# A tuned single-core hybrid layer: operand splits moved, the first norm's outputs shared with POOL, and the last sum kept in PSUM

## The chip, the cores and the metric

The kernel runs on one core of a Trainium2 chip. The metric is the device time of one execution in microseconds (us). Of the kernel before, three runs gave 1477.32, 1479.01 and 1482.19 us; the median is 1479.01. Engines are named as in the profile: PE is TensorE (PEld its weight load), DVE is VectorE, ACT is ScalarE, POOL is GpSimd, SP is SyncE, which here issues DMAs.

## The reference

One post-norm layer on x of 1024 tokens by 2048 channels, all in float32:

```python
h = einsum('bsd,dc->bsc', x, w_in) + b_in                   # 2048 -> 4352 columns
q, k, v, g_attn, u_pool, g_pool = split(h)                  # 1024, 128, 128, 1024, 1024, 1024
a = banded_sink_attention(q, k, v, sinks, bias, valid) * silu(g_attn)   # 16 heads of 64, 2 kv heads, window 128
b = multiscale_pool(u_pool, w_pool, pool_scale) * silu(g_pool)          # trailing means over 2, 4, 8, 16
mix = einsum('bsc,cd->bsd', concatenate([a, b]), w_out)     # 2048 -> 2048
ple = sigmoid(einsum('bsd,de->bse', x, w_gate_ple)) * einsum('bsp,pd->bsd', p, w_ple)
out = layer_norm(DEEPNORM_ALPHA * x + mix + ple, ln_gain, ln_bias)
```

The three large products (34 blocks of 128 columns for `w_in`, 16 for `w_gate_ple`, 16 for `w_out`, each over 2048 channels) are nearly all of the arithmetic. `ple` is a per-layer embedding: p has 256 channels.

## The kernel before

**Layout.** Everything is kept transposed: channels on the 128 partitions, tokens along the free axis, in two halves of 512 tokens.

**Products.** A float32 operand is split into a high part (a cast on ACT, `copy`, L728) and a low part (a subtraction on DVE, `lo`, by the helper at L125). A product is then three matmuls, high by high, low by high and high by low (`mm3`, L182 to L184). A weight of 128x512 split this way is a unit (`wh`, `wl`), made four ahead of its use from a ring of five raw tiles.

**Jobs.** The large products run as Strassen-like jobs, each for two blocks of outputs and half of the contraction. A job has seven smaller products over the operands `b11`, `b21`, `t1`, `t2`, `t3`, `b22`, `t4` (h for high, l for low); the t operands are sums and differences of raw blocks (`two`), built on DVE. Results gather in `part` tiles: ACT copies the first product of a bank (L402), DVE adds the others from the PSUM banks `qa`, `qb` and `sc`. Two or three jobs share one set of operands and are a group; a product of one job is 12 matmuls of 512 columns. The operands of a group come from `set_from` (raw x), from `set_kept` (differences kept in DRAM), or from other sums.

**The order of the work.** `run_group` runs the products of a group one after another; each is a step of a clock. `after(n, f)` and `later(n, f)` place a piece of work n ticks on, and the scheduler then puts the instructions into each engine's queue. So a tick sets the place in a queue and not a time.

**The stages.** s1 to s4 are the projections from x, in which the heads of the attention run beside s2. The first group of s1 runs while x and the first weights are still being loaded; the embedding products of four early blocks (`EARLY`) stand among its products: `ple_split(n)` splits a block's embedding weights into `t3h` and `t3l` (L767), p lies split in `t4h` and `t4l`, and `ple_half(n, h)` is a turn of 12 matmuls, six in each of the banks `tr` and `pv`, whose results ACT copies to `b22h` or `b22l` as storage. `v_build` (L522) brings the values V, fetched from DRAM, to the form that the attention needs, with transposes on PE. s5 is the output projection for 768 tokens; s6 is eight plain jobs (`run_plain`, units a11 to a22, no Strassen) for the other 256, with operands split from `rest_x`.

**The norm.** Weights of `w_out` are centred over output channels, and `less_mean` (L905) adds what is left of the mean, so that the norm needs only the mean of squares. `norm_square` squares a block on ACT (L915), `norm_sums` adds squares with PE (L924), `norm_scale` forms the reciprocal root, which matmuls with ones spread over the partitions (L931 in `norm_spread` for the 768 tokens, L957 for the 256), and `norm_out` multiplies each of 16 blocks by it on DVE, scales and shifts it on ACT (`ident_act`, L128) and stores it. The first norm (`one`, 768 tokens) runs beside s6. The second (`two`, 256 tokens) ends the kernel: `norm_out_two` (L975) does two blocks at a time.

**Queues.** Loads go through SP (`load`, L139) and stores and other DMAs through POOL (`aside`, L144). POOL also does the masks (L612), some softmax additions, and accumulating DMAs (L415).

Of the kernel before, what the change touches and what calls it, by code (L numbers as in the profile page):

```python
# [64 lines left out]
class Layer:  # L65
# [265 lines left out]
    def set_kept(self, get, keep):  # L331

        r = {}

        def fetch(i):
            if i < 7:
                u = UNITS[BESIDE[i]]
                h, k = int(u[2:] or 1) - 1, 2 * (int(u[1]) - 1)
                r[u] = []
                for n in range(2):  # L340
                    src = keep[u][n] if u in keep else get(h, k + n)
                    r[u] += [self.fetch(src[:, m]) for m in range(2)]

        def step(i):
            u = UNITS[BESIDE[i]]
            self.split_unit(u, r.pop(u))
            fetch(i + 2)

        def begin():
            self.F = T  # L350
            fetch(0)
            fetch(1)

        return [begin] + [lambda i=i: step(i) for i in range(7)]
# [123 lines left out]
    def run_plain(self, g):  # L478

        (job,), order = self.groups[g]  # L480
        for i in range(2):
            ps = self.bank(BANKS[0][i], 2)[:, :F2]
            for u in range(2):
                wh, wl = self.take()
                for k in range(4):
                    f = slice(k * P, (k + 1) * P)
                    mm = self.mm3(ps, (wh[:, f], wl[:, f]), self.x_plain(4 * u + k), u + k == 0, False)
                if u:
                    mm = self.less_mean(ps, F1)
                self.mark("PE", mm)  # L490
                self.feed_raw()
                if u:
                    t = self.new_part(job.b[i])
                    self.add_to(t, ps, False)
                    job.done(job.b[i], t)
# [18 lines left out]
    def v_build(self, g, src):  # L514
# [12 lines left out]
        for h in range(2):  # L527
            self.ident_act(src[h], src[h], self.c(C_BIN + VB))
            self.after(2 + (1 + 4 * g) * h, lambda h=h: build(h))
# [240 lines left out]
    def ple_half(self, n, h, tags):  # L770

        i = EARLY[n]
        if n > 1 and not h:
            self.ple_split(n)
# [184 lines left out]
    def norm_out(self, L, j):  # L959
        d = L["d"].pop(j)  # L960
        self.tt(d, d, L["a"], ALU.mult)
        self.ident_act(d, d, self.c(C_B + j), self.c(C_G + j))
# [19 lines left out]
    def run(self):  # L982
# [77 lines left out]
        s6 = [Job(w, b0, b1, 0, None, lambda b, c: self.second_done(b, c), F2, plain=True) for w, b0, b1 in centred]  # L1060
        for j in s4[-2:]:
            j.wait = 6
# [42 lines left out]
        def first(fetch, r):  # L1105
# [11 lines left out]
            piece(s1[2], 0, up)  # L1117
            fetch("b12")
# [3 lines left out]
            self.ple_load(3)  # L1122
# [21 lines left out]
        self.run_group(0, steps, before=lambda *at: at in turn and self.ple_half(*turn[at], (("tr", 1), ("pv", 1))))  # L1144
# [22 lines left out]
        def build_kv(b, build, group):  # L1167
            src = [self.slot()[:, :T] for h in range(2)]
            for h in range(2):
# [9 lines left out]
        self.after(t + 63 + 22, lambda: build_kv(VB, self.v_build, 1))  # L1179
# [116 lines left out]
        self.first_done = first_done  # L1296
        for i in range(n5):
            self.run_group(g + i)
# [3 lines left out]
        hi, lo = ([self.tile(self.xp[u], [P, 4, half], f"{u}{s}", F32R).rearrange("p k t -> p (k t)") for u in ("b11", "b21")] for s in "hl")  # L1302
        for k in range(4):
            r = rest_x[k]
            f = slice((k % 2) * 2 * F2, (k % 2) * 2 * F2 + 2 * F2)
            h, l = (t[k // 2][:, f].rearrange("p (k t) -> p k t", k=2) for t in (hi, lo))
            nc.scalar.copy(out=h, in_=r)
            self.lo(l, r, h)
# [28 lines left out]
        self.later(3, lambda: self.norm_scale(one, 2))  # L1337
        for j in range(NB):
            self.later(6 + 18 * j // 16, lambda j=j: self.norm_out(one, j))
# [4 lines left out]
        for i, d in enumerate(pair):  # L1344
            self.norm_out_two(two, 2 * i, d, (nc.gpsimd, None, nc.gpsimd, nc.vector, nc.gpsimd, None, nc.gpsimd, nc.vector)[i])
# [55 lines left out]
```

## Time and profile before

| view | number |
|---|---|
| median of the runs | 1479.01 us |
| profiled execution | 1477.94 us, span 1476.2 us |
| PE busy | 1439.7 us, 98% of the span |
| DVE busy | 1123.1 us, 76% |
| ACT busy | 788.4 us, 53% |
| POOL busy | 295.8 us, 20% |
| mean granted clock of PE | 0.993 |

A row of the timeline has the start, the duration, the engine, the line, the operation, output and inputs by their names, the shape, a count, and in brackets how long the engine had been idle before it and what released it. A row of the waits has what waited for what, the sum of the waits, their number and the longest. Short rows of one engine overlap a little at their ends, since they are pipelined.

### The profile page before, as it was taken

How to read it: one execution, taken by the hardware profiler on the slowest of the kernel's cores; microseconds unless marked ns; L12 is line 12 of the kernel's file. 1: busy time of each engine (PE TensorE's matmuls, PEld its weight loads, DVE VectorE, ACT ScalarE, POOL GpSimd, SP SyncE). 2: the span in 40 equal slices, each digit the busy share in tenths (PEclk: the TensorE clock that was granted, in tenths of full speed). 3: DMA queues.
4: the chain of work that ended last, by engine and by line, in shares of the span. 5: the costliest groups of instructions: out<-in, count | busy, mean ns of one | idle time of the engine just before them, and what ended most of it. 6: DMA issues, size and time to landing. Idle time of an engine off the chain costs nothing. (4 is left out here: it accounts for less than half of the span.)

```text
span 1476.2 us, 20532 instructions
## 1 busy us (share of the span) xinstructions
PE 1439.7 (98%) x6928; PEld 1217.1 (82%) x6928; DVE 1123.1 (76%) x2033; ACT 788.4 (53%) x1566; POOL 295.8 (20%) x412
## 2 busy tenths in 40 slices
PE   8899999999999999999999999999999999999996
PEld 7788888888888788888788778788877888899995
DVE  6758577888788888888777786767678566987786
ACT  6535456655666566565655354433356433554475
POOL 1000113233233232324011111111011111111232
PEclk9899999999999999999999999999999999999998
DMA  9364687454445554466765759899699678595465
GB/s 350 145 215 170 164 230 232 145 170 165 158 173 181 185 169 171 172 214 218 205 198 133 207 160 307 288 266 289 196 320 301 168 190 231 138 258 126 120 239 200
DMA packets 109993, 301.35 MB, mean 204 GB/s; under 512 B 12544, under 2 KB 18048, under 8 KB 109888
## 3 DMA queue, kind: packets, MB, share of 16 engines
q1 hardware_dynamic: 84672, 217.46, 42.9%
q0 software_dynamic: 21888, 75.25, 21.0%
q10 hardware_dynamic: 3328, 7.34, 1.5%
q8 instruction: 54, 0.88, 0.2%
q14 instruction: 51, 0.42, 0.1%
HBM read 205.62 MB, written 94.37 MB: 203 GB/s over the span
## 5 line engine op out<-in xcount | busy, mean ns | idle before, releaser
L728 ACT CAST wh<-raw 128x512 fp32r<-128x512 f32 x428 | 264.1, 619 | 401.5 <-PE qa L183 132.5
L125 DVE TENSOR_TENSOR wl<-raw,wh 128x512 fp32r<-128x512 f32 x428 | 300.3, 705 | 111.2 <-ACT wh L728 105.4
L402 ACT COPY part<-qa 128x512 f32<-128x512 f32 (+1 forms) x180 | 103.9, 577 | 75.0 <-PE qa L184 74.0
L612 POOL TENSOR_SCALAR_AFFINE_SELECT s<-s 128x512 fp32r<-128x512 f32 x128 | 102.1, 809 | 132.2 <-ACT s L605 96.6
L125 DVE TENSOR_TENSOR part<-part,qb 128x512 f32<-128x512 f32 (+1 forms) x120 | 81.0, 675 | 44.9 <-PE qb L184 38.7
L182 PE MATMUL qa<-b11h,wh 128*128 128x512 f32 (+2 forms) x292 | 109.3, 374 | 0.4 <-ACT wh L728 0.4
L182 PE MATMUL qb<-b21h,wh 128*128 128x512 f32 (+2 forms) x292 | 109.1, 374 | 0.0
L184 PE MATMUL qa<-b11h,wl 128*128 128x512 f32 (+2 forms) x292 | 108.9, 373 | 0.0
L183 PE MATMUL qa<-b11l,wh 128*128 128x512 f32 (+2 forms) x292 | 108.8, 373 | 0.0
L184 PE MATMUL qb<-b21h,wl 128*128 128x512 f32 (+2 forms) x292 | 108.7, 372 | 0.0
L183 PE MATMUL qb<-b21l,wh 128*128 128x512 f32 (+2 forms) x292 | 108.5, 372 | 0.0
L182 PE MATMUL qa<-t2h,wh 128*128 128x512 f32 (+1 forms) x260 | 100.9, 388 | 3.3 <-ACT wh L728 2.1
L182 PE MATMUL qb<-t1h,wh 128*128 128x512 f32 (+1 forms) x260 | 101.2, 389 | 2.3 <-ACT t2h L728 1.4
L182 PE MATMUL qa<-t4h,wh 128*128 128x512 f32 (+1 forms) x260 | 100.4, 386 | 2.4 <-DVE part L125 2.4
L182 PE MATMUL qa<-t3h,wh 128*128 128x512 f32 (+1 forms) x260 | 100.6, 387 | 1.8 <-ACT part L402 1.8
L184 PE MATMUL qa<-t2h,wl 128*128 128x512 f32 (+1 forms) x260 | 100.1, 385 | 1.6 <-DVE wl L125 1.6
L182 PE MATMUL qb<-b22h,wh 128*128 128x512 f32 (+1 forms) x260 | 100.2, 386 | 0.0
L183 PE MATMUL qb<-t1l,wh 128*128 128x512 f32 (+1 forms) x260 | 100.0, 385 | 0.0
L184 PE MATMUL qb<-t1h,wl 128*128 128x512 f32 (+1 forms) x260 | 100.0, 385 | 0.0
L184 PE MATMUL qb<-b22h,wl 128*128 128x512 f32 (+1 forms) x260 | 99.8, 384 | 0.0
L183 PE MATMUL qa<-t3l,wh 128*128 128x512 f32 (+1 forms) x260 | 99.7, 384 | 0.0
L183 PE MATMUL qb<-b22l,wh 128*128 128x512 f32 (+1 forms) x260 | 99.7, 383 | 0.0
(325 smaller groups left out, 3577.1 us busy)
## 6 DMA issues: line engine op xcount, KB each, us to landing
raw<-in_win SPq DMA_DIRECT2D x65, 512.0 KB, 4.3
h<-part SPq DMA_DIRECT2D x34, 512.0 KB, 2.9
part<-h POOLq DMA_DIRECT2D x34, 512.0 KB, 6.6
cw<-in_wout SPq DMA_DIRECT2D x64, 256.0 KB, 3.0
raw<-in_wgate SPq DMA_DIRECT2D x32, 512.0 KB, 4.9
raw<-wc SPq DMA_DIRECT2D x32, 512.0 KB, 4.4
s<-in_x SPq DMA_DIRECT2D x44, 256.0 KB, 5.6
wc<-cw SPq DMA_DIRECT2D x32, 256.0 KB, 2.4
```

Source lines behind the costliest of these rows:

```text
L125: return (eng or self.nc.vector).tensor_tensor(out=out, in0=a, in1=b, op=op)
L182: mm(ps, wh, xh, start=start, stop=False, skip_group_check=True)
L183: mm(ps, wh, xl, start=False, stop=False, skip_group_check=True)
L184: return mm(ps, wl, xh, start=False, stop=stop, skip_group_check=True)
L402: self.mark("ACT", self.nc.scalar.copy(out=dst, in_=ps))
L612: nc.gpsimd.affine_select(out=o4, in_=a4, pattern=[[0, 4], [sign, P]], compare_op=ALU.is_ge, fill=0.0, base=0 if side else -1, channel_mul ...
L728: ins = self.nc.scalar.copy(out=out, in_=a)
```

## The change

Seven edits stand in one diff:

- **A, early units.** The 512 KB load for the early blocks 2 and 3 is issued ahead of the loads of `b12`, the raw weights and `b22`, and `ple_split(2)` and `ple_split(3)` are issued before the second product of the first group, not at the turns that use them.
- **B, values.** V of the second kv group is fetched and transposed in two halves, at 17 and 24 ticks; before, both were fetched at 22.
- **C, operand steps.** In `set_kept` a step other than the first splits two of its four pieces at once, and the other two, with the fetch of a later operand, a tick later.
- **D, last operand.** The operand of s6 is split during the last group of s5, piece by piece, and not after it.
- **E, first norm.** `norm_scale`'s second argument, the ticks from it to the matmuls that spread the reciprocal root (`norm_spread`), is 3 instead of 2; the outputs come at 7 + 17j // 16 instead of 6 + 18j // 16, and the scale and shift of odd blocks are one POOL instruction each (128x768) where ACT had one.
- **F, last sum.** In the last plain job the second block's partial sum is added to PSUM by a matmul with the identity; ACT squares from PSUM and DVE copies it out, where DVE added the partial sum first.
- **G, last outputs.** In `norm_out_two` the odd blocks are all scaled and shifted by POOL, where POOL had four, DVE two and ACT two of them.

```diff
@@ set_kept
         def step(i):
             u = UNITS[BESIDE[i]]
-            self.split_unit(u, r.pop(u))
-            fetch(i + 2)
+            pieces = r.pop(u)
+            self.split_unit(u, [])
+            for n in range(2):
+                self.split_part(u, n, pieces[n])
+            def rest():
+                for n in range(2, 4):
+                    self.split_part(u, n, pieces[n])
+                fetch(i + 2)
+            if i:
+                self.after(1, rest)
+            else:
+                rest()
@@ run_plain
+            final = job.mean and i
...
+                if final and not u:
+                    t = self.new_part(job.b[i])
+                    nc.tensor.matmul(ps, self.ident, t, start=False, stop=False, skip_group_check=True)
                 if u:
                     mm = self.less_mean(ps, F1)
...
-                if u:
+                if u and final:
+                    job.done(job.b[i], ps)
+                    nc.vector.tensor_copy(out=t, in_=ps)
+                elif u:
                     t = self.new_part(job.b[i])
                     self.add_to(t, ps, False)
                     job.done(job.b[i], t)
@@ v_build
-        for h in range(2):
+        for h in src:
             self.ident_act(src[h], src[h], self.c(C_BIN + VB))
-            self.after(2 + (1 + 4 * g) * h, lambda h=h: build(h))
+            self.after(2 + h * (g == 0), lambda h=h: build(h))
@@ ple_half
-        if n > 1 and not h:
-            self.ple_split(n)
@@ norm_out
         self.tt(d, d, L["a"], ALU.mult)
-        self.ident_act(d, d, self.c(C_B + j), self.c(C_G + j))
+        if j % 2:
+            self.nc.gpsimd.tensor_scalar(out=d, in0=d, scalar1=self.c(C_G + j), scalar2=self.c(C_B + j), op0=ALU.mult, op1=ALU.add)
+        else:
+            self.ident_act(d, d, self.c(C_B + j), self.c(C_G + j))
@@ the first loads
+            self.ple_load(3)
             fetch("b12")
             for job in s1[1:3]:
                 piece(job, 1, all_)
             fetch("b22")
-            self.ple_load(3)
@@ the first group
-        self.run_group(0, steps, before=lambda *at: at in turn and self.ple_half(*turn[at], (("tr", 1), ("pv", 1))))
+        def early(*at):
+            if at in turn:
+                self.ple_half(*turn[at], (("tr", 1), ("pv", 1)))
+            elif at == (1, 0):
+                self.ple_split(2)
+                self.ple_split(3)
+        self.run_group(0, steps, before=early)
@@ beside s2
-        self.after(t + 63 + 22, lambda: build_kv(VB, self.v_build, 1))
+        for h in range(2):
+            self.after(t + 63 + 17 + 7 * h, lambda h=h: build_kv(VB, self.v_build, 1, (h,)))
@@ s5
+        def last_operand(k):
...
+            nc.scalar.copy(out=h, in_=rest_x[k])
+            self.lo(l, rest_x[k], h)
         for i in range(n5):
+            if i == n5 - 1:
+                for k in range(4):
+                    self.later(5 + 2 * k, lambda k=k: last_operand(k))
             self.run_group(g + i)
-        for k in range(4):
...
-            nc.scalar.copy(out=h, in_=r)
-            self.lo(l, r, h)
@@ s6 and the norms
-        self.later(3, lambda: self.norm_scale(one, 2))
+        self.later(3, lambda: self.norm_scale(one, 3))
         for j in range(NB):
-            self.later(6 + 18 * j // 16, lambda j=j: self.norm_out(one, j))
+            self.later(7 + 17 * j // 16, lambda j=j: self.norm_out(one, j))
...
-            self.norm_out_two(two, 2 * i, d, (nc.gpsimd, None, nc.gpsimd, nc.vector, nc.gpsimd, None, nc.gpsimd, nc.vector)[i])
+            self.norm_out_two(two, 2 * i, d, nc.gpsimd)
```

In the first group, DVE's queue around the split `t3l` stands so before (`two` and `raw` are sums of operand blocks and weights, `t1l` the low part of operand t1, `wl` a weight's):

```order
L125 TENSOR_TENSOR raw_298<-raw_297,raw_298 128x512
L125 TENSOR_TENSOR wl_577<-s_212_571,wh_576 128x512
L125 TENSOR_TENSOR raw_297<-s_212_571,raw_297 128x512
L125 TENSOR_TENSOR t3l_338<-two_334,t3h_337 128x512
L125 TENSOR_TENSOR raw_297<-raw_297 128x512
L125 TENSOR_TENSOR two_325<-two_331,two_325 128x1024
L125 TENSOR_TENSOR wl_623<-raw_293,wh_622 128x512
L125 TENSOR_TENSOR t3l_338<-two_334,t3h_337 128x512
L125 TENSOR_TENSOR two_523<-two_330,two_308 128x1024
```

and with the change, up to the first half of the sum for t2 (`two_527`):

```order
L125 TENSOR_TENSOR b21l_458<-two_319,b21h_457 128x1024
L125 TENSOR_TENSOR wl_482<-raw_295,wh_481 128x512
L125 TENSOR_TENSOR t3l_338<-two_324,t3h_337 128x512 x2
L125 TENSOR_TENSOR two_308<-two_326,two_308 128x1024
L125 TENSOR_TENSOR wl_500<-raw_297,wh_499 128x512
L125 TENSOR_TENSOR two_309<-two_327,two_309 128x1024
L125 TENSOR_TENSOR t1l_522<-two_308,t1h_521 128x1024
L125 TENSOR_TENSOR raw_293<-raw_293 128x512
L125 TENSOR_TENSOR t1l_522<-two_309,t1h_521 128x1024
L125 TENSOR_TENSOR wl_535<-s_183_443,wh_534 128x512
L125 TENSOR_TENSOR two_527<-two_332,two_308 128x1024
```

Both halves of `t3l` moved from behind the weight work of the third product to ahead of the sums for t1.

On POOL, behind the reciprocal root of the first norm (`st`), there were only the DMAs of the outputs (`d`, two for each block):

```order
L125 TENSOR_TENSOR st_13467<-st_13467,mhalf 128x6
L144 DMA out<-d_12195 128x512
L144 DMA out<-d_12195 128x256
L144 DMA out<-d_12196 128x512
L144 DMA out<-d_12196 128x256
L144 DMA out<-d_12197 128x512
```

and now each odd block has its scale and shift there too:

```order
L125 TENSOR_TENSOR st_13467<-st_13467,mhalf 128x6
L144 DMA out<-d_12195 128x512
L144 DMA out<-d_12195 128x256
L981 TENSOR_SCALAR d_12196<-d_12196,cst 128x768
L144 DMA out<-d_12196 128x512
L144 DMA out<-d_12196 128x256
L144 DMA out<-d_12197 128x512
```

Eight such instructions of 128x768 stand in POOL's queue, the last in front of the last output of the first norm.

On PE, in s2, the transposes of V (`sc<-ident`) stood at the end of the product over t4, in front of the next group's `b11`:

```order
L184 MATMUL qa_4684<-t4h_1509,wl_4789 128x512
L603 MATMUL tr_4909<-ident,s_4552 128x128 x2
L603 MATMUL tr_4909<-ident,s_4627 128x128 x2
L522 MATMUL sc_4934<-ident,s_4760 128x128 x4
L182 MATMUL qa_4948<-b11h_1273,wh_4829 128x512
```

and now those of the first half stand in front of the product over t2, some 80 rows earlier:

```order
L184 MATMUL qb_4712<-b21h_1279,wl_4605 128x512
L587 MATMUL sc_4737<-kh_1759,s_4674 128x256
L587 MATMUL sc_4737<-kl_1760,s_4674 128x256
L587 MATMUL sc_4737<-kh_1759,s_4675 128x256
L587 MATMUL sc_4737<-kl_1760,s_4675 128x256
L542 MATMUL sc_4744<-ident,s_4577 128x128 x4
L182 MATMUL qa_4687<-t2h_1377,wh_4642 128x512
```

More of the change, by code (lines that the diff above doesn't have):

```diff
@@ L478, in run_plain @@
     def run_plain(self, g):
+        nc = self.nc
         (job,), order = self.groups[g]
@@ L1060, in run @@
         s6 = [Job(w, b0, b1, 0, None, lambda b, c: self.second_done(b, c), F2, plain=True) for w, b0, b1 in centred]
+        s6[-1].mean = True
         for j in s4[-2:]:
@@ L1165, in run, with build_kv @@
         self.kv = self.work_pool("kv", 1, over)
-        def build_kv(b, build, group):
-            src = [self.slot()[:, :T] for h in range(2)]
-            for h in range(2):
+        def build_kv(b, build, group, halves=(0, 1)):
+            src = {h: self.slot()[:, :T] for h in halves}
+            for h in halves:
                 self.aside(src[h], kvd[b][:, h * T : h * T + T])
@@ L1296, in run @@
         self.first_done = first_done
+        hi, lo = [], []
+        def last_operand(k):
+            if k % 2 == 0:
+                for t, s in ((hi, "h"), (lo, "l")):
+                    u = ("b11", "b21")[k // 2]
+                    t.append(self.tile(self.xp[u], [P, 4, half], f"{u}{s}", F32R).rearrange("p k t -> p (k t)"))
+            f = slice((k % 2) * 2 * F2, (k % 2) * 2 * F2 + 2 * F2)
+            h, l = (t[k // 2][:, f].rearrange("p (k t) -> p k t", k=2) for t in (hi, lo))
+            nc.scalar.copy(out=h, in_=rest_x[k])
+            self.lo(l, rest_x[k], h)
         for i in range(n5):
+            if i == n5 - 1:
+                for k in range(4):
+                    self.later(5 + 2 * k, lambda k=k: last_operand(k))
             self.run_group(g + i)
         g += n5
-        hi, lo = ([self.tile(self.xp[u], [P, 4, half], f"{u}{s}", F32R).rearrange("p k t -> p (k t)") for u in ("b11", "b21")] for s in "hl")
-        for k in range(4):
-            r = rest_x[k]
-            f = slice((k % 2) * 2 * F2, (k % 2) * 2 * F2 + 2 * F2)
-            h, l = (t[k // 2][:, f].rearrange("p (k t) -> p k t", k=2) for t in (hi, lo))
-            nc.scalar.copy(out=h, in_=r)
-            self.lo(l, r, h)
         self.x_plain = lambda k: tuple(t[k // 4][:, (k % 4) * F2 : (k % 4) * F2 + F2] for t in (hi, lo))
```

## The prediction

> **What bounds the kernel now.** First the page's head, then the waits, then PE's timeline at each long wait, last the busy times in short windows.
>
> ```profile
> span 1476.2 us, 20532 instructions
> PE 1439.7 (98%) x6928; PEld 1217.1 (82%) x6928; DVE 1123.1 (76%) x2033; ACT 788.4 (53%) x1566; POOL 295.8 (20%) x412
> ...
> PE tr L184 <- DVE t3l L125: 5.3, 1, 5.3
> PE tr L182 <- ACT t3h L767: 2.3, 1, 2.3
> PE pv L625 <- DVE v L125: 1.7, 1, 1.7
> ```
>
> PE is busy for 1439.7 of 1476.2 us, so this change can win only PE's idle time (36.5 us), the clock lost beside it, and the tail; three single waits are 9.3 us of it. It loses wherever another engine, late, makes PE wait. The two longest waits stand in the first group, with a slowed clock behind them:
>
> ```profile
> 33.09 0.39 PE L184 MATMUL sc<-b21h,wl 128*128 128x512 f32 x1
> 35.75 0.50 PE L182 MATMUL tr<-t4h,t3h 128*128 128x512 f32 x1 [2.28 <-ACT t3h L767]
> 42.26 0.80 PE L184 MATMUL tr<-t4h,t3l 128*128 128x512 f32 x1 [5.31 <-DVE t3l L125]
> 60.40 0.39 PE L182 MATMUL tr<-t4h,t3h 128*128 128x512 f32 x1
> 63.12 0.39 PE L182 MATMUL qa<-t2h,wh 128*128 128x512 f32 x1
> ...
> 36.00:40.00 4.00, 0.95 (x4) 0.42 (x3) 4.00 (x8) 0.91 (x3) 1.46 (x1) 0.70 0.59 199
> 40.00:44.00 4.00, 1.74 (x4) 1.46 (x5) 4.00 (x7) 0.45 (x1) 0.00 (x0) 0.50 0.00 0
> 44.00:48.00 4.00, 4.00 (x11) 3.10 (x11) 3.93 (x5) 2.42 (x4) 0.00 (x0) 0.52 0.52 210
> ```
>
> A window row has the stretch, its length, the busy time (and count) of PE, PEld, DVE, ACT and POOL, then PE's granted clock, the DMA share and GB/s. The clock's mean over 36 to 40 is 0.70 and over the next 4 us 0.50: full for (0.70 - 0.50) / 0.50 x 4 = 1.6 us, then half, so it fell at 37.6. By the same working it rose 0.2 us before 48. That is 10.2 us at half speed, begun 4.1 us after the steady work ended at 33.5.
>
> **A, the early units** (`ple_split(2)` and `(3)` sooner, the 512 KB load for them ahead of b12). Before, DVE is full up to 44, and t3l is one of its last steps:
>
> ```profile
> 26.21 1.23 DVE L125 TENSOR_TENSOR two<-two,two 128x1024 f32<-128x1024 f32 x1 [3.02 <-DMA two<-in_x]
> 29.70 2.36 DVE L125 TENSOR_TENSOR t1l<-two,t1h 128x1024 fp32r<-128x1024 f32 x2
> 41.52 0.68 DVE L125 TENSOR_TENSOR t3l<-two,t3h 128x512 fp32r<-128x512 f32 x1
> ...
> 27.47 1.05 ACT L728 CAST t1h<-two 128x1024 fp32r<-128x1024 f32 x1 [2.29 <-DVE two L125]
> 44.80 0.59 ACT L728 COPY b22h<-tr 128x512 f32<-128x512 f32 x1 [4.35 <-PE tr L184]
> ...
> GB/s 350 145 215 170 164 230 232 145 170 165 158 173 181 185 169 171 172 214 218 205 198 133 207 160 307 288 266 289 196 320 301 168 190 231 138 258 126 120 239 200
> ```
>
> On SP's queue the load is moved past b12, the raw weights of two jobs and b22. It lands where b12 did, at 26.2, and each of those lands one slot later, 524 KB at the first slice's 350 GB/s, 1.5 us. DVE had stood idle for b12 for 3.02 us; now the t3l pair runs from 26.8 to 28.0, and that covers the slot (b12 is there at 27.7). So t3h and t3l are ready long before 33.3. The price is a later t2: from 26.21 up to its second half DVE's new queue holds ten 128x512 steps and six of 128x1024. Back to back a row's span overlaps the next by about 0.08, which leaves 0.60 of 0.68 and, for the two t1l, 2.28 / 2 = 1.14: 6.0 + 6.8 = 12.8, up to 39.05.
>
> PE then runs: p2 ends at 33.1 + 0.2 = 33.3 (matmuls stream every 2.72 / 12 = 0.227 us, from 60.40 to 63.12). Four turns of 12 early matmuls and three jobs of the third product are 7 x 2.72 = 19.1. Two waits stay: the first job's bank, which DVE's `part<-part,qb` frees at 36.2 (0.2), and the second turn's bank `tr`: its copy stands on ACT behind the cast of t2's second half, 39.05 + 1.05 + 0.59 = 40.7, where PE asks at 36.2 + 2.7 = 38.95 (1.75). The fourth product starts at 33.3 + 19.1 + 0.2 + 1.75 = 54.4 instead of 63.12: **-8.7**. Weights don't bound that stretch: the units are made four ahead, 4 x 2.7 us, and raw lands 1.5 us later. Bounds: 33.3 + 19.1 = 52.4 gives -10.7; if 1.75 us of idling drops the clock once more for 10.2 us, half of that goes, 5.1: -3.6.
>
> The trace has 2.28 idle us, 1.2 us of matmuls, and the second wait from 42.26 - 5.31 = 36.95; the clock fell 0.65 us into that one. The Trainium skill, page "TensorE: Matmul & The Clock Gate", section "Part 1: The HAM clock gate", has the clock halved after an idle window of about 3.4 us; the trace agrees no further than that 4.1 us with little work were enough. By that rule 1.75 us would not trip it.
>
> **B, values** (halves of V fetched at ticks 17 and 24, not both at 22; transposes about 80 PE rows earlier) and **C, operand steps** (two pieces now, two a tick later):
>
> ```profile
> 489.24 0.47 PE L625 MATMUL pv<-s,v 128*128 128x256 f32 x2 [1.75 <-DVE v L125]
> ...
> 705.21 0.68 DVE L125 TENSOR_TENSOR part<-part,qb 128x512 f32<-128x512 f32 x1
> 706.04 0.47 PE L182 MATMUL qb<-t1h,wh 128*128 128x512 f32 x1 [1.38 <-ACT t2h L728]
> ```
>
> B: 80 matmuls at 0.227 are 18 us, ten times the wait, so v is there: **-1.75**. The transposes themselves stand on PE ahead of that stretch's products; if their source comes late they stop those, and the bound is 0. C: the cast named is long done; the bank is free when the DVE row above ends at 705.89. In the new order one 128x512 step (0.60) fewer stands ahead of it: **-0.65** (0 to -1.4).
>
> **D, last operand** split during the group before. ACT and DVE do the same eight steps earlier, in a stretch where PE's waits are short:
>
> ```profile
> 1387.68 0.44 PE L182 MATMUL qb<-t1h,wh 128*128 128x384 f32 x1 [0.82 <-DVE d L125]
> ```
>
> By the new order PE comes to this wait without two matmuls of 384 columns that had run ahead (2 x 0.227 x 384 / 512 = 0.34), and the bank comes about as late, perhaps 0.1 sooner: **+0.2** (-0.8 to +1).
>
> **E, the first norm.** All 16 outputs are multiplied on DVE; the scale and shift of the eight odd ones go from ACT to POOL, in place, 128x768 in SBUF. That stretch:
>
> ```profile
> 1421.00:1434.00 13.00, 13.00 (x112) 13.00 (x112) 12.99 (x22) 12.27 (x20) 6.34 (x12) 1.00 0.81 275
> 1434.00:1450.00 16.00, 15.51 (x125) 14.71 (x124) 16.00 (x28) 14.99 (x23) 8.90 (x17) 1.00 0.98 356
> ...
> 1444.86 0.68 DVE L125 TENSOR_TENSOR wl<-raw,wh 128x512 fp32r<-128x512 f32 x1
> 1445.59 0.38 PE L184 MATMUL qb<-b11h,wl 128*128 128x256 f32 x1
> ```
>
> DVE is the bound here, not ACT: it is busy for 28.99 of 29 us, and PE takes `wl` 0.05 us after DVE writes it (1445.54, 1445.59). So ACT's eight steps fewer gain nothing (27.3 of 29 us busy, it keeps pace), and a microsecond that DVE loses is one that PE loses. On POOL's queue each step stands ahead of the DMA issues of its output, for which no engine waits. DVE's own work stays; but POOL costs DVE time where both read SBUF:
>
> ```profile
> 318.53 0.75 POOL L125 TENSOR_TENSOR s<-s 128x256 f32<-128x256 f32 x1 [6.88 <-ACT s L583]
> 319.51 0.91 POOL L125 TENSOR_TENSOR s<-s 128x256 f32<-128x256 f32 x1 [0.23 <-ACT s L583]
> 318.79 1.04 DVE L125 TENSOR_TENSOR wl<-raw,wh 128x512 fp32r<-128x512 f32 x1
> 319.75 0.69 DVE L125 TENSOR_TENSOR st<-st 128x2 f32<-128x2 f32 x1
> ```
>
> The DVE subtraction, 0.68 elsewhere, lasts 1.04 beside the first POOL step, and a step of 128x2 lasts 0.69, up to where the second ends (320.42, 320.44). They take turns. What such a POOL step takes itself:
>
> ```profile
> 1466.69 0.56 POOL L975 TENSOR_SCALAR t1h<-t1h,cst 128x256 f32<-128x256 f32 x1 [2.64 <-DVE t1h L125]
> 1.18 0.29 POOL masks.py:199 TENSOR_SCALAR_AFFINE_SELECT ident<-ident 128x128 f32<-128x128 f32 x1
> 455.30 0.64 POOL L612 TENSOR_SCALAR_AFFINE_SELECT s<-s 128x512 fp32r<-128x512 f32 x1 [1.27 <-ACT s L605]
> 34.50 2.95 POOL L1153 TENSOR_SCALAR b<-cst 128x8 f32<-128x8 f32 x1 [13.74 <-DMA cst<-in_cst]
> ```
>
> Between 128x128 and 128x512 a step grows by 0.35 / 384 = 0.9 ns an element; from 0.56 for 128x256 that is 0.56 + 512 x 0.0009 = 1.02 for 128x768. Of the two rows above, DVE lost 0.36 of 0.75 and 0.54 (0.69 less 0.15) of 0.91, half to six tenths. What DVE does right behind an odd multiplication is a subtraction of two SBUF operands every time, so I take eight tenths, 0.81, and seven of the eight steps (the last falls where DVE is no longer full): **+5.7**. Bounds: nothing lost, less the 0.39 before L931's first matmul, if the spread a tick later finds its input: -0.4; each step three times the 0.56, 1.67, all of it lost: 8 x 1.67 = +13.4.
>
> The Trainium skill, page "SBUF — State Buffer", section "SBUF: two separate sides", speaks against this edit: a GpSimd step that reads SBUF and a DVE step with two SBUF inputs exclude each other for a whole instruction. The two pairs agree that they take turns. Whole instructions, 8 x 1.02 = 8.2, would make the sum below -3.3.
>
> **F and G, the end.** The last block's mean-centred part is added by an identity matmul into PSUM, ACT squares from there; all eight odd final outputs on POOL, even ones on ACT.
>
> ```profile
> 1417.89 1.56 PE L931 MATMUL sc<-q,ones 128*128 128x512 f32 x4 [0.39 <-ACT q L948]
> 1461.46 0.42 DVE L125 TENSOR_TENSOR t1h<-t1h,qb 128x256 f32<-128x256 f32 x1 [1.56 <-PE qb L905]
> 1461.97 0.42 ACT L915 ACTIVATE t2l<-t1h 128x256 f32<-128x256 f32 x1 [2.53 <-DVE t1h L125]
> 1465.82 1.88 DVE L125 TENSOR_TENSOR t1h<-t1h,sc 128x512 f32<-128x512 f32 x3 [1.31 <-PE sc L957]
> 1470.85 1.08 ACT L128 ACTIVATE t2h<-t2h,cst 128x256 f32<-128x256 f32 x2
> ```
>
> Gone from the path: DVE's addition with its handover, 1461.97 - 1461.46 = 0.51. Added: one f32 matmul with 256 columns; L931's take 1.56 / 4 = 0.39 each, so 0.4 is taken. POOL's eight steps of 0.56 keep pace with DVE's multiplications (1.88 / 3, about 0.60 a pair of blocks, one operand in PSUM), and ACT's last step now ends after eight of its own rather than ten, 0.5 sooner. **-0.6** (-1.5 to +0.8).
>
> **The sum**: -8.7 - 1.75 - 0.65 + 0.2 + 5.7 - 0.6 = -5.8 on the profiled execution's 1477.94 (span 1476.2 and 1.7 around it): 1472.1. The runs' median, 1479.01, is 1.07 above that: **1473.2**.
>
> **Rivals.**
>
> 1. POOL costs DVE nothing: E's term is -0.4 in place of +5.7, the sum -11.9, 1467.1. For it: POOL works 15.2 us of those 29 already, PE loses 0.5 there, and the `wl` at 1444.86 keeps its 0.68. Against: the stretched rows at 318.79 and 319.75.
> 2. POOL's 128x768 step is dear and DVE waits for all of it: 8 x 1.67 = 13.4, the sum +1.9, 1480.9: slower. It decides from (5.8 + 5.7) / 8 = 1.44 us a step. For it: 2.95 us for 128x8 at 34.50 shows that a step of this kind can take far more than its size; against: 0.56 at 1466.69.
> 3. The early units' wait only moves: PE still stands 1.75 us, the clock falls, 5.1 come back: the sum -0.7, 1478.3. For it: the fall after 2.28 + 0.65 idle us; against: 2.7 us of work on either side of the stall.
>
> **Chances.** Forecast 51%, rival 1 25%, rival 2 12%, rival 3 12%. The measurement tells 0.3%, 4.4 us, from no change: faster is below 1474.6. The forecast's own range is 1470 to 1477, with six tenths of it faster; rival 1 is faster, rival 3 the same, rival 2 two thirds the same. Faster 0.51 x 0.6 + 0.25 = 0.56; slower 0.04, and 0.02 for dearer steps (at 2.95 each, 8 are +23.6, the sum +12.1); same 0.38. The range holds rival 1 at its foot and rival 2's near side: 1466 to 1480.
>
> **What would show it.** A: no wait on t3l, one wait of about 1.75 for `tr` near 39, full clock from 36 to 48, `qa<-t2h` at 54.4; a clock of 0.5 there is rival 3. B, C: no wait at `pv<-s,v`; 0.7 at `qb<-t1h`. E: eight POOL steps of about 1.0, DVE rows beside them stretched by 0.8, and PE idle for some 6 us (0.5 before) between 1421 and 1450 of the old times; unstretched rows are rival 1, steps over 1.44 rival 2. F: `qb L905` to the first square under 0.3. The forecast is wrong if the kernel lands outside 1470 to 1477, and its reasons are wrong if A or E is off by over 3 us even where the sum fits.

## The result

The changed kernel takes 1471.44 us (median of 8 runs, 1468.64 to 1473.43) against 1476.33 us for the kernel before (8 runs, 1472.72 to 1482.19). The ratio is 0.9959, with a 95% interval of 0.9946 to 0.9972: a time 0.41% shorter. The medians differ by 4.9 us, and the two profiled spans by 4.5 us; the prediction had 5.8. The three runs of the kernel before that were shown at first (median 1479.01) lay a little high, so the predicted 1473.2 stands beside 1471.4.

The page's head after:

```profile
span 1471.7 us, 20536 instructions
PE 1438.8 (98%) x6930; PEld 1216.1 (83%) x6930; DVE 1125.4 (76%) x2031; ACT 780.2 (53%) x1556; POOL 307.2 (21%) x424
```

PE's work is the same as before within 1 us, so what changed is its idle time and its clock. In the view of PE's waits, the rows that were not there or were far shorter before:

```profile
PE qb L182 <- DVE d L125: 2.0, 1, 2.0
...
PE tr L182 <- ACT b22h L748: 1.4, 1, 1.4
PE sc L587 <- DVE s L125: 1.4, 5, 0.4
```

The 5.3 and the 2.3 us for `t3l` and `t3h` and the 1.7 for `v` are gone from it. PE's timeline in the first group, and its windows there:

```profile
36.01 0.47 PE L182 MATMUL qb<-t1h,wh 128*128 128x512 f32 x1 [0.65 <-DVE part L125]
...
40.41 0.50 PE L182 MATMUL tr<-t4h,t3h 128*128 128x512 f32 x1 [1.44 <-ACT b22h L748]
...
54.15 0.39 PE L182 MATMUL qa<-t2h,wh 128*128 128x512 f32 x1
...
36.00:40.00 4.00, 2.96 (x12) 2.15 (x12) 4.00 (x7) 2.13 (x4) 0.00 (x0) 1.00 0.68 241
40.00:44.00 4.00, 3.58 (x16) 2.98 (x17) 4.00 (x8) 3.55 (x8) 0.00 (x0) 1.00 0.23 91
44.00:48.00 4.00, 4.00 (x19) 3.33 (x18) 4.00 (x5) 1.52 (x3) 1.11 (x2) 1.00 0.63 255
```

Two waits of 0.65 and 1.44 us are left, the granted clock is 1.00, and the fourth product starts at 54.15 instead of 63.12. The longer wait ends with a copy on ACT that stands behind the cast of t2's second half, and that one waits for DVE's sum:

```profile
37.58 1.22 DVE L125 TENSOR_TENSOR two<-two,two 128x1024 f32<-128x1024 f32 x1
...
38.83 1.04 ACT L748 CAST t2h<-two 128x1024 fp32r<-128x1024 f32 x1 [1.64 <-DVE two L125]
39.78 0.58 ACT L748 COPY b22h<-tr 128x512 f32<-128x512 f32 x1
```

Since PE does the same matmuls in nearly the same order, the start of one matmul in one trace can be taken from its start in the other. How that difference moves from place to place tells where time was won and lost (times of the kernel before, us):

| stretch | what of the change lies in it | moved by | predicted |
|---|---|---|---|
| 0 to 63 | A, early units | -9.0 | -8.7 |
| 63 to 484 | nothing | +0.3 | 0 |
| 484 to 650 | B, values | -0.2 | -1.75 |
| 650 to 708 | C, operand steps | -0.8 | -0.65 |
| 708 to 1376 | nothing | +1.6 | 0 |
| 1376 to 1416 | D, last operand | +1.8 | +0.2 |
| 1416 to 1424 | E, spread of the first norm moved | -0.7 | 0 |
| 1424 to 1459 | E, POOL's steps | +3.3 | +5.7 |
| 1459 to the end | F and G (identity matmul +0.4, tail -1.2) | -0.8 | -0.6 |
| sum | | -4.5 | -5.8 |

### The profile page after: what moved, and what is told of

The parts are those of the page before. It is cut to its first block, busy times and chain, and to the rows that moved or that the text cites. A ratio compares the mean times of both kernels' runs of the same rounds, so it can differ in the third digit from the quotient of the medians.

```text
span 1471.7 us, 20536 instructions
## 1 busy us (share of the span) xinstructions
PE 1438.8 (98%) x6930; PEld 1216.1 (83%) x6930; DVE 1125.4 (76%) x2031; ACT 780.2 (53%) x1556; POOL 307.2 (21%) x424
## 5 line engine op out<-in xcount | busy, mean ns | idle before, releaser
L125 DVE TENSOR_TENSOR wl<-raw,wh 128x512 fp32r<-128x512 f32 x428 | 301.2, 707 | 100.4 <-ACT wh L748 97.4
L125 DVE TENSOR_TENSOR part<-part,qb 128x512 f32<-128x512 f32 (+1 forms) x120 | 81.1, 676 | 46.0 <-PE qb L184 41.7
L184 PE MATMUL qa<-t4h,wl 128*128 128x512 f32 (+1 forms) x260 | 99.7, 384 | 0.0
L184 PE MATMUL qa<-t3h,wl 128*128 128x512 f32 (+1 forms) x260 | 99.6, 383 | 0.0
```

The costliest lines, as they stand in the source:

```text
L125: return (eng or self.nc.vector).tensor_tensor(out=out, in0=a, in1=b, op=op)
L184: return mm(ps, wl, xh, start=False, stop=stop, skip_group_check=True)
```

## The experiments

Twelve runs were made: nine kernels (e1 to e9), and a second profile each of the kernel before, of the change and of e4 (e10 to e12). The theory at the start: A's gain is whole and stays, POOL's steps cost PE what DVE loses, and D's loss is a clock that falls behind a stall. For each run the table has the same differences against the first profile of the kernel before; the ratios are against the kernel before on the same chip.

| run | ratio, interval | span | at 300 | 484-650 | 690-708 | 708-1376 | 1376-1416 | 1424-1459 |
|---|---|---|---|---|---|---|---|---|
| the change | 0.9959, 0.9946-0.9972 | 1471.7 | -9.0 | -0.2 | -0.7 | +1.6 | +1.8 | +3.3 |
| e1 first norm on ACT | 0.9946, 0.9926-0.9966 | 1470.2 | -9.1 | +0.6 | -1.1 | +4.7 | +0.2 | +0.4 |
| e2 operand as before | 0.9962, 0.9950-0.9974 | 1469.1 | -9.3 | -0.7 | -1.0 | +1.7 | +0.1 | +3.3 |
| e3 both undone | 0.9938, 0.9921-0.9954 | 1465.0 | -9.5 | -0.6 | -1.1 | +1.5 | -0.2 | +0.3 |
| e4 early units alone | 0.9944, 0.9927-0.9961 | 1464.3 | -10.1 | -0.7 | -0.5 | -0.3 | +0.4 | 0.0 |
| e5 POOL a third | one run | 1469.5 | -9.1 | -0.6 | -0.7 | +2.9 | +0.1 | +2.3 |
| e6 steps undone | one run | 1472.2 | -9.1 | +0.4 | -0.5 | +1.6 | +1.7 | +3.3 |
| e7 values undone | one run | 1467.8 | -9.0 | -0.9 | -1.1 | +0.1 | +0.4 | +3.4 |
| e8 turns later | 0.9934, 0.9920-0.9948 | 1464.1 | -10.3 | -1.2 | -1.1 | +1.4 | -0.2 | +0.4 |
| e9 without values | 0.9941, 0.9921-0.9961 | 1469.7 | -10.6 | +2.2 | -1.1 | +4.2 | -0.2 | +0.3 |
| e10 before again | one run | 1476.3 | -1.1 | -0.2 | -0.5 | +2.2 | 0.0 | 0.0 |
| e11 the change again | one run | 1471.5 | -8.6 | -0.9 | -1.1 | +3.7 | 0.0 | +3.4 |
| e12 early units again | one run | 1470.4 | -9.0 | -0.9 | -0.5 | +4.6 | -0.2 | 0.0 |

A single span is a poor judge here: e4 and e12 are one kernel and differ by 6.1 us, of which 4.9 arise between 708 and 1376. The differences of one stretch repeat far better, to 0.1 us between 1424 and 1459. The intervals of e1 to e4, e8 and e9 all overlap that of the change, so what one edit is worth is read from the stretches and not from the ratios.

### e1: POOL's steps back on ACT

```diff
-        if j % 2:
-            self.nc.gpsimd.tensor_scalar(out=d, in0=d, scalar1=self.c(C_G + j), scalar2=self.c(C_B + j), op0=ALU.mult, op1=ALU.add)
-        else:
-            self.ident_act(d, d, self.c(C_B + j), self.c(C_G + j))
+        self.ident_act(d, d, self.c(C_B + j), self.c(C_G + j))
```

> The changed kernel with the scale and shift of all 16 outputs of the first norm on ACT again; the later ticks stay. In the changed kernel five of the eight POOL steps (1.36 us each) stand beside a DVE multiplication of 1.41 instead of 0.95 us, and the other three beside a stretched row too; together DVE loses 3.7 us there. Theory (POOL and DVE take turns, DVE bounds this stretch): all multiplications take 0.95, and PE's offset against the kernel before grows by 0.3 or less between the first and the last s6 job where it grew by 3.3; the span is about 1468.4, 3.3 under the changed kernel's 1471.7. Rival (ACT was the bound, and POOL's help is worth its price): the DVE rows shrink, but PE now waits for ACT's casts of the weights (wh), and the span stays at 1471.7 or grows.

The stretch moved by +0.4 instead of +3.3; the span fell only by 1.5, because this execution lost 4.7 us between 708 and 1376. The DVE groups of the changed kernel between 1410 and 1452 (group rows: busy, mean ns of one, idle before):

```profile
L125 DVE TENSOR_TENSOR wl<-raw,wh 128x512 fp32r<-128x512 f32 x23 | 16.6, 729 | 0.1
L125 DVE TENSOR_TENSOR d<-d,sq 128x768 f32<-128x768 f32 x10 | 10.8, 1078 | 0.0
L125 DVE TENSOR_TENSOR part<-part,sq 128x768 f32<-128x768 f32 x6 | 7.1, 1177 | 0.0
```

and of this run:

```profile
L125 DVE TENSOR_TENSOR wl<-raw,wh 128x512 fp32r<-128x512 f32 x26 | 17.5, 680 | 0.1
L125 DVE TENSOR_TENSOR d<-d,sq 128x768 f32<-128x768 f32 x10 | 9.5, 946 | 0.0
L125 DVE TENSOR_TENSOR part<-part,sq 128x768 f32<-128x768 f32 x6 | 5.7, 944 | 0.0
...
1425.00:1441.00 16.00, 15.59 (x128) 14.97 (x127) 16.00 (x28) 15.11 (x24) 9.49 (x18) 1.00 0.96 336
```

DVE had lost 23 x 0.049 + 10 x 0.132 + 6 x 0.233 = 3.8 us, and PE gets 3.0 of it back. With all 16 steps ACT is busy for 15.1 of 16 us, and PE does not wait for it more than before: ACT needed no help. The theory holds for this stretch, and the rival falls; by the ratios alone the two kernels can't be told apart.

### e2 and e3: the last operand's split as before, alone and with e1

```diff
-            if i == n5 - 1:
-                for k in range(4):
-                    self.later(5 + 2 * k, lambda k=k: last_operand(k))
             self.run_group(g + i)
...
+        for k in range(4):
+            r = rest_x[k]
...
+            nc.scalar.copy(out=h, in_=r)
+            self.lo(l, r, h)
```

> The changed kernel with the split of s6's operand where it was, behind the last s5 group. In the changed kernel PE stands 2.02 us at one point ahead of the t1 product of that group, and the next twelve matmuls take 0.32 us apart instead of 0.175 (1.45 us). Theory (a stall of 2 us in one piece drops the granted clock, two shorter ones do not): two t2 matmuls run ahead again, waits of about 0.5 and 0.8, no slow matmuls behind, and about 1.9 us less: span 1469.8. Rival (the bank is late because of the accumulating DMA ahead of it, whatever the order of the split): one wait of about 2 and the slow matmuls stay, span 1471.7.

> The changed kernel without the POOL steps of the first norm and without the earlier split of s6's operand. Theory: both gains add, 3.3 + 1.9: span about 1466.5, faster than both kernels. Rival: only one of them shows, 1468 to 1470, since the operand's split then falls into the stretch where DVE is full.

In both the stretch from 1376 to 1416 is back to about 0 (+0.1, -0.2). The kernel before has two waits there (the second stands in the prediction):

```profile
1386.24 0.44 PE L182 MATMUL qa<-t2h,wh 128*128 128x384 f32 x1 [0.52 <-ACT wh L728]
```

What had happened in the changed kernel, in PE's timeline and its windows:

```profile
1379.66 0.41 PE L182 MATMUL qb<-t1h,wh 128*128 128x384 f32 x1 [2.02 <-DVE d L125]
...
1379.60:1383.40 3.80, 3.74 (x13) 3.77 (x14) 3.80 (x6) 1.45 (x4) 0.00 (x0) 0.58 0.00 0
```

and the same place in e1, which has the same order of instructions there:

```profile
1382.53 0.41 PE L182 MATMUL qb<-t1h,wh 128*128 128x384 f32 x1 [1.79 <-DVE d L125]
...
1382.50:1386.00 3.50, 3.47 (x20) 3.50 (x21) 3.50 (x6) 1.79 (x4) 0.00 (x0) 1.00 0.00 0
```

With the clock at 1.00 the edit costs 0.2 us, as predicted; with it at 0.58 for the next 3.8 us it costs 1.8. So the loss of D above 0.2 us or so is the clock's, in those executions in which it falls. In e2 the two `t2` matmuls run ahead and the waits are 0.63 and 0.82, as its theory has it. By its runs e2 gains nothing on the change, though (0.9962 against 0.9959): what the edit costs on the mean of many executions is not shown. e3 adds the two gains up: its span of 1465.0 is 1.5 below what was expected.

### e4: the early units alone

```diff
             piece(s1[2], 0, up)
+            self.ple_load(3)
             fetch("b12")
...
             fetch("b22")
-            self.ple_load(3)
...
+        def early(*at):
+            if at in turn:
+                self.ple_half(*turn[at], (("tr", 1), ("pv", 1)))
+            elif at == (1, 0):
+                self.ple_split(2)
+                self.ple_split(3)
```

> The kernel before with the early units' part alone: the load ahead of b12, and the two splits ahead of the second product. Theory: the fourth product starts 9.0 us sooner (54.15 instead of 63.12, as in the changed kernel), full clock from 36 to 48, and all of it stays to the end: span 1467.2, runs 9 us under the kernel before, so faster than the whole change. Rival (later stages give back what comes early, by transfers that now collide): under 6 us at the end, span over 1470.

At 300 this kernel is 10.1 us ahead (9.0 when profiled again as e12), at the end 11.9 (5.8 in e12). By its runs it is 0.56% faster than the kernel before, and the whole change 0.41%, with intervals that overlap: A alone is, by these runs, worth no less than the whole. The end of e12, 5.8 us and a span of 1470.4, is what the rival foresaw (under 6, over 1470); it lies in the stretch from 708 to 1376, for which see e10 to e12.

### e5: POOL's steps at a third of their size

```diff
-            self.nc.gpsimd.tensor_scalar(out=d, in0=d, ...
+            self.nc.gpsimd.tensor_scalar(out=d[:, :256], in0=d[:, :256], ...
```

> The changed kernel, but the eight POOL steps of the first norm scale and shift only the first 256 of 768 columns (the other 512 columns of the odd blocks stay without gain and bias, so this output is not the layer's). Order and number of instructions stay. In the changed kernel a POOL step begins while DVE subtracts (0.68), shows 1.36 us, and the DVE multiplication behind the addition from PSUM shows 1.41 instead of 0.95. Theory (they take turns by instruction; what DVE loses is POOL's own time less the 0.33 us of the addition from PSUM that lies beside it): POOL's own time is 0.46 + 0.33 = 0.79 for 768 columns and falls to about 0.4 for 256, so the multiplications show 1.0 to 1.05, and PE's offset grows by under 0.8 between the first and the last s6 job, not by 3.3. Rival (a fixed price for each handover, whatever the size): the multiplications stay at 1.4 and PE's offset grows by 3.3.

POOL's and DVE's timelines at one of the steps, first of the changed kernel:

```profile
1428.58 1.35 POOL L981 TENSOR_SCALAR d<-d,cst 128x768 f32<-128x768 f32 x1
...
1428.40 0.68 DVE L125 TENSOR_TENSOR wl<-raw,wh 128x512 fp32r<-128x512 f32 x1
1429.00 0.41 DVE L125 TENSOR_TENSOR t1l<-t1l,qa 128x256 f32<-128x256 f32 x1
1429.33 1.41 DVE L125 TENSOR_TENSOR d<-d,sq 128x768 f32<-128x768 f32 x1
```

POOL's 1.35 begins inside a DVE subtraction, which keeps its 0.68 and ends at 1429.08. From there to POOL's end, 1429.93, are 0.85 us: that is POOL's own time. The addition from PSUM keeps its 0.41 beside it. The multiplication, with two SBUF operands, shows 1.41 instead of 0.95. In e5:

```profile
1425.53 1.62 POOL L981 TENSOR_SCALAR d<-d,cst 128x256 f32<-128x256 f32 x1
...
1425.86 0.95 DVE L125 TENSOR_TENSOR d<-d,sq 128x768 f32<-128x768 f32 x1
1426.73 0.96 DVE L125 TENSOR_TENSOR wl<-raw,wh 128x512 fp32r<-128x512 f32 x1
```

A step a third as large shows a longer span, 1.62, since it now waits for a whole multiplication (to 1426.81) and then takes 0.34 (to 1427.15); the subtraction behind it shows 0.28 more than its 0.68. So both sides of the expectation missed on DVE's loss: it is neither 0.05 to 0.1 nor 0.46 but 0.28 a step, and PE's stretch moved by 2.3, not by under 0.8 and not by 3.3. POOL's own time did fall with the size (0.85 to 0.34 for 768 and 256 columns, 1.0 ns a column), as the theory has it. But the row of DVE that stands beside the step changed with it: no PSUM addition covers it now. What DVE loses depends on POOL's own time and on which DVE instruction has its turn beside it. A POOL row's length tells little of this, because it holds the wait.

### e6 and e7: the operand steps and the values undone, one at a time

```diff
         def step(i):
             u = UNITS[BESIDE[i]]
-            pieces = r.pop(u)
-            self.split_unit(u, [])
...
+            self.split_unit(u, r.pop(u))
+            fetch(i + 2)
```

> The changed kernel with the operand steps of set_kept as before (all four pieces at once). Theory: PE's wait ahead of qb<-t1h near 696 is 0.6 to 0.9 us longer than the changed kernel's 0.64, and nothing else moves, since the order of all queues is the same from there to the last s5 group; the waits near 920 and 1140 that the changed kernel has longer than the kernel before (2.2 us together) come from when transfers land and may or may not be there. Rival (the steps' new order makes those waits): near 920 and 1140 PE's offset no longer grows.

```diff
-        for h in range(2):
-            self.after(t + 63 + 17 + 7 * h, lambda h=h: build_kv(VB, self.v_build, 1, (h,)))
+        self.after(t + 63 + 22, lambda: build_kv(VB, self.v_build, 1))
```

> The changed kernel with V of the second kv group fetched and transposed at once as before. Theory: the wait of 1.4 to 1.75 us before pv<-s,v near 480 is back, but the small waits for softmax sums behind it (0.2 to 0.4 each, five in the changed kernel) go, so that PE's offset near 530 is 0.3 to 1.3 us behind the changed kernel's. Rival (the edit gains nothing): the same offset near 530 within 0.2.

C: between 690 and 708 the profiles with the edit moved by -0.7 to -1.1, those without it (e4, e6, e10, e12) by -0.5, and the first profile of the kernel before is the 0. So the edit is worth some 0.2 to 0.6 us, and the first profile of the kernel before had this wait somewhat long. The wait that e6 was to lengthen by 0.6 to 0.9 us is 0.88 there and 0.64 in the change: its theory had the size wrong. B: the wait is back in e7,

```profile
480.30 0.35 PE L645 MATMUL pv<-s,v 128*128 128x256 f32 x1 [1.64 <-DVE v L125]
```

and with the edit it is gone, but the changed kernel has others, near 489 and 638 above all, in the view of waits `PE sc L587 <- DVE s L125`, 1.4 us in five, where the kernel before has 0.3 in one. By 650 e7 stands 0.9 us ahead of its place at 484, the changed kernel 0.2. The expected place, 530, showed 0.36 us between the two: e7 there is 8.95 ahead, the change 9.31. Over a longer stretch nothing of it is left. The waits near 920 and 1140, in the changed kernel about 2.2 us longer together than in the kernel before, which the two runs were also to explain, do not go with the edits one at a time: e6 loses nothing near 920 and all of its part near 1140, e7 gains near 920 and loses near 1140.

### e8: the turns later

```diff
-        turn = {(2, 0): (2, 0), (2, 1): (2, 1), (2, 2): (3, 0), (3, 0): (3, 1)}
+        turn = {(2, 0): (2, 0), (2, 2): (2, 1), (3, 0): (3, 0), (3, 1): (3, 1)}
```

(on e3)

> The changed kernel without the POOL steps and the earlier operand split, and with the second to fourth turn of the early blocks one product of a job later each. In the changed kernel the second turn waits 1.44 us for its PSUM bank, whose copy stands on ACT behind the cast of t2's second half. Theory: that copy is done at 40.4, PE comes to the second turn at 41.6, the wait is gone, and the fourth product starts 1.4 us sooner, offset about -10.9 against the kernel before at 63; all of it stays: span 1463.6. Rival (the wait moves to the banks of the third product's second job, or to ACT's casts): the fourth product starts no sooner, span 1465.

PE reaches the second turn at 42.0 and does not wait:

```profile
42.03 0.39 PE L182 MATMUL tr<-t4h,t3h 128*128 128x512 f32 x1
```

In e3 that wait had ended at 39.90 after 0.72; it differs from one execution to the next (1.44 in the change and in e11, none in e4 and e12), with the time at which PE comes to it and that at which the bank is free. So against e3 0.7 was to be had and 0.8 came (-10.3 against -9.5 at 300). The same turn now stands behind the fourth product's start, so that this matmul alone (50.2) tells nothing. The span is 1464.1, the ratio 0.9934, the lowest of all: this version is faster than the kernel before by 0.66%, and by its ratio 0.25% below the changed kernel, with intervals that just meet.

### e9 to e12: the values once more, and three kernels a second time

```diff
-        for h in range(2):
-            self.after(t + 63 + 17 + 7 * h, lambda h=h: build_kv(VB, self.v_build, 1, (h,)))
+        self.after(t + 63 + 22, lambda: build_kv(VB, self.v_build, 1))
```

(e9, on e8; the other three are the kernels named, unchanged)

> The kernel of the run with later turns (no POOL steps, no earlier operand split), and V of the second kv group fetched and transposed at once as before. Over the runs so far, PE's offset moved between 484 and 650 by -0.34 us on the mean in the six with the change of V and by -0.78 in the two without it. Theory (the wait that the edit takes away comes back as waits for softmax sums): no difference within 0.5 us, span 1463.5 to 1464.5. Rival (it wins its 1.75 and other causes hid it): 1 to 1.75 us slower, span 1465 to 1466.

> The kernel before, profiled a second time, for how much a stretch moves from one execution to the next. In the runs with both the change of V and that of the operand steps, PE lost 1.4 to 4.7 us between 708 and 1376, in a stretch where all queues hold the same work in the same order; in the others -0.3, 0.1 and 1.6. Theory (chance: when transfers land): this second profile differs from the first by 1 us or more in that stretch. Rival (the edits cause it): within 0.5 us.

> The changed kernel, profiled a second time. Theory: its loss between 708 and 1376 is another than 1.6 us by 1 us or more; the early gain is again 9.0 to 9.1 us, the first norm's loss 3.3; the stall ahead of t1 near 1379 is again 1.7 to 2.1 us, and the clock falls only if it is over 1.95, since in four runs it fell at 1.96, 2.02 and (elsewhere) 2.25 and not at 1.72 to 1.93. Rival (the fall comes by chance, whatever the length): the clock falls at under 1.9 or stays at over 2.0.

> The kernel before with the early units' part alone, profiled a second time. Theory (chance): a loss between 708 and 1376 other than the first profile's -0.3 by 1 us or more. Rival (no loss without the other edits): within 0.5 us of it.

e9 is 1.4 us slower than e8 by the medians, with intervals that overlap widely. Its profile lost 2.2 us between 484 and 650 where the others without B won: its wait of 1.80 for `v` was followed by a fallen clock.

```profile
478.70:482.00 3.30, 3.30 (x12) 2.81 (x13) 2.77 (x8) 2.20 (x9) 2.06 (x3) 0.60 0.52 178
```

Without that fall B is worth nothing that these profiles show; with it, 2 to 3 us (+2.2 here against -0.4 on the mean of the eight with the edit). Whether the runs have it often is open.

The second profiles settle the stretch from 708 to 1376: the kernel before moved by +2.2 against itself, the change by +3.7 where it had +1.6, the early units alone by +4.6 where they had -0.3. The order of work there is the same on all engines. The places are the same in each: PE's waits near 920 and 1140, the first behind DVE's sums from `cc`, which wait for a DMA. Of the kernel before, the second time:

```profile
930.18 0.50 PE L182 MATMUL qa<-t4h,wh 128*128 128x512 f32 x1 [1.57 <-DVE part L125]
```

where the first had 1.16, and in e12 it is 2.19. So none of the edits is needed for it. What sets when those transfers land was not tried.

e11 answers on the clock too: its stall ahead of t1 was 1.50 us, and the clock stayed; but one of 2.32 near 921 left it at 1.00 as well:

```profile
921.50:925.00 3.50, 3.35 (x15) 2.75 (x16) 3.50 (x7) 0.28 (x1) 0.44 (x1) 1.00 1.00 393
```

## Why the prediction was right

The sign, the size and the main terms held: -5.8 predicted, -4.9 by the medians. It is right by offsetting errors in the smaller terms, though, which the table of stretches shows.

**A, -8.7: right in its mechanism and size** (-9.0; in e4, e11 and e12 -10.1, -8.6 and -9.0). The bank `tr` was to hold PE for 1.75 until 40.7; it held it for 1.44 until 40.4. DVE's `part` step was to hold the first job until 36.2, and PE went on at 36.0. The clock stayed full, so rival 3 fell at this place. e8 takes the second turn's wait away. Against the second profile of the kernel before, which is 1.1 us ahead at 300, the gain is 7.5 to 9.0: its clock was at half for 6.8 us and not for 10.2, so a part of this term is the luck of the first profile.

**E, +5.7: the mechanism right, the price too high.** DVE is the bound, POOL and DVE take turns, ACT's relief is worth nothing: e1 shows each. The failing step is "eight tenths, 0.81, and seven of the eight steps". Measured, a step in the steady part costs DVE 0.46 us, DVE loses 3.8 us in all and PE 3.0 (3.3 less the 0.3 that remains without POOL). Two things were not in it: POOL's own time is 0.85 and not 1.02, and an addition from PSUM stands between the subtraction and the multiplication, under which 0.4 us of POOL's time pass at no cost. Rival 1, which asked for unstretched rows, fell; rival 2 needed a step over 1.44, which the rows seem to come near with 1.35, but half a microsecond of that is POOL's wait. The spread a tick later won 0.7, while the working had left it as a mere bound of 0.4. The wait before L931 is gone; counted from start to start it had cost 0.55 (0.67 us from the matmul before it, where 0.12 is usual), and the next product starts 1.09 us after the spread's first matmul where it was 1.20.

The Trainium skill, page "SBUF — State Buffer", section "SBUF: two separate sides", was the ground for its stronger price, whole instructions, 8.2 us. The trace agrees that a DVE instruction with two SBUF operands waits (1.41 us for 0.95), and the PSUM row at 1429.00, unstretched at 0.41 beside POOL, agrees with the condition that this page puts; the price of whole instructions is too high here by the covered part.

**D, +0.2: right without the clock, +1.8 with it.** The step that failed is "and the bank comes about as late". It did, but the order turned two waits (0.52 and 0.82) into one of 1.5 to 2.0 in the six profiles that have the edit, and in two of them (2.02 and 1.96) the clock fell behind it. The prediction had looked for that fall at A alone.

**B, -1.75: wrong.** The failing step is "v is there", as if nothing else were due. The wait for `v` did go, but in each of the eight profiles with the edit PE then waits for softmax sums near 489, which none of the six without it does:

```profile
488.90 0.33 PE L587 MATMUL sc<-kh,s 128*128 128x128 f32 x1 [0.27 <-DVE s L125]
...
489.62 0.33 PE L587 MATMUL sc<-kh,s 128*128 128x128 f32 x1 [0.28 <-DVE s L125]
```

Over the whole trace such waits are 1.4 us here against 0.3 before, but in the second profiles 0.5 in both, so they are not all of the account; what else takes the gain back was not traced to its end. Between 484 and 650 the eight profiles with the edit average -0.4, the four others besides e9 -0.7 against the first profile of the kernel before. **C, -0.65:** right in direction, some 0.2 to 0.6 by comparison with the second profiles.

**F and G, -0.6: about right.** The identity matmul cost 0.4, as worked out. ACT's square begins 0.1 after the matmul of `less_mean` (L923 now) ends; under 0.3 was the mark:

```profile
1457.85 0.28 PE L923 MATMUL qb<-two,w 128*128 128x256 f32 x1
1458.23 0.38 ACT L933 ACTIVATE t2l<-qb 128x256 f32<-128x256 f32 x1 [2.50 <-PE qb L923]
...
1460.78 0.70 PE L975 MATMUL sc<-t2l,ones 128*128 128x256 f32 x2 [1.51 <-DVE t2l L125]
```

The last of these rows stood so in the kernel before:

```profile
1464.56 1.22 PE L957 MATMUL sc<-t2l,ones 128*128 128x256 f32 x2 [1.51 <-DVE t2l L125]
```

The tail behind 1461 won 1.2 us, of which 0.5 is the clock: the last spread shows 0.70 here where the kernel before had 1.22 (and 0.70 in its second profile), and e2 and e8, with 1.22, won 0.7.

**Not in the sum:** +1.6 between 708 and 1376, which lies within what e10 to e12 show one kernel to move by from one execution to the next (2.1 to 4.9). The first profile of the kernel before was a kind one there. Two profiles of one kernel (e4, e12) differ in this stretch by 4.9 us, as much as the whole gain; so the runs' medians and the places that repeat carry the verdict, and not two spans.

## What to carry to other kernels

Where the bound is one engine, compare the starts of the same instruction in two traces along the program: gains and losses of several edits fall apart by place, and a total that fits can hide two wrong terms. Work given to an idle engine is not free if its steps and those of the engine that binds hold each other up, as POOL's and DVE's did here: look at the rows of the binding engine beside it, and leave such work with an engine that is busy but does not bind, here ACT. Profile the same kernel twice before reading a few microseconds out of a stretch that waits for transfers.

## What the runs showed of the hardware

**The clock can fall behind stalls of about 2 us, and where the stall lies matters as well as its length.** It fell to half, to 0.56 to 0.66 on the mean of some 3.5 us, behind stalls of 1.80 (e9), 1.96 (e6), 2.02 (the change) and 2.25 us (e2), and stayed behind 1.79 and 1.93 (e1), 1.91 (e5, e7), 2.19 (e12), 2.32 (e11) and 2.33 (e9). So the length alone does not decide in that range; a limit of 1.95, which was expected from the first eight runs, fell with e9 to e12. At D a fall costs about 1.5 us (+1.8 and +1.7 with it, 0.0 to +0.4 without).

The traces hold more than the lengths. Within each of the fourteen, the changes of the clock lie whole steps of 3.413 us apart: it was at half for one step in e2, e6, e9 and the change, for two in the first group of e10 and for three in that of the kernel before (6.8 and 10.2 us). Cut along these steps, the stall of 2.02 in the change lies within one, while that of 2.32 in e11 (917.78 to 924.61) crosses into the next:

```profile
1376.76:1380.17 3.41, 1.39 (x9) 1.10 (x8) 2.89 (x6) 2.51 (x5) 0.00 (x0) 1.00 0.00 0
1380.17:1383.59 3.42, 3.42 (x13) 3.42 (x12) 3.35 (x5) 1.07 (x3) 0.00 (x0) 0.50 0.00 0
1383.59:1387.00 3.41, 3.41 (x21) 3.41 (x20) 2.72 (x5) 0.80 (x2) 0.94 (x2) 1.00 0.00 0
...
917.78:921.19 3.41, 1.55 (x7) 0.94 (x5) 3.38 (x6) 0.00 (x0) 1.43 (x3) 1.00 0.63 191
921.19:924.61 3.42, 2.96 (x13) 2.44 (x14) 3.42 (x7) 0.00 (x0) 0.57 (x2) 1.00 1.02 390
```

So take every step in which the clock was full, up to the end of s6. The clock fell after each of the five in which PE was busy for 1.45 us or less, after one of the seven with 1.55 to 1.70 (1.61, e9), and after none with more. This is read from the traces; no run shifted a stall on purpose to test it.

The Trainium skill, page "TensorE: Matmul & The Clock Gate", section "Part 1: The HAM clock gate (the "warmup" mystery)", speaks of an idle window of 3.4 us and of a window that runs free of the program. The steps agree with the length of the window and with its running free; that only a gap over 3.4 us would count does not agree with these rows, where a stall of 1.80 was enough.

**A POOL step's row contains its wait for DVE.** 128x256 showed 1.62 us and 128x768 showed 1.35, with own times of 0.34 and 0.85. The row of a DVE step with two SBUF operands beside it holds its wait as well (1.41 for 0.95), and the addition with one operand in PSUM holds none (0.41).
